# A hybrid two-layer trunk on one core: two matmul stages read last column first, spatial weights interleaved, pooling matmuls halved

## The chip, the core and the metric

The kernel runs on one core of a Trainium2 chip. The metric is the device time of one execution in microseconds (us); lower is better. The engines are TensorE (PE, with its weight loads shown apart as PEld), VectorE (DVE), ScalarE (ACT), GpSimd (POOL) and SyncE (SP), which issues most of the transfers.

## The reference

The input is 512 positions by 1024 features. Two layers follow, each a mixer and a gated FFN with residuals, then a last normalisation. Cut to what matters:

```python
# layer 0
proj = rms_norm(h, norm_mix[0]) @ w_in_even              # 1024 -> 2048
a_b, a_c, a_v, z_b = split(proj, 4)                      # 512 each
y_a = a_b * causal_dwconv3(a_c * a_v, conv_a)
y_b = multiscale_pool(z_b, w_pool, pool_scale)           # 4 groups x (128 -> 128)
h = h + concat(y_a, y_b) @ w_out_even
h = h + gated_conv_ffn(rms_norm(h, norm_ffn[0]), ...)    # 1024 -> 2816 -> 1024
# layer 1
proj = gelu(rms_norm(h, norm_mix[1]) @ w_in_odd)         # 1024 -> 2 x 1024: u, v
ws = w_spatial * tril(ones(128, 128))                    # 8 heads x 128 x 128
gate = einsum('hts,bnshc->bnthc', ws, rms_norm(v, sgu_norm)) + b_spatial
h = h + (u * gate) @ w_out_odd
h = h + gated_conv_ffn(rms_norm(h, norm_ffn[1]), ...)
return rms_norm(h, final_norm)
```

The gated FFN is `silu(conv3(x @ w_gate) + b) * (x @ w_up) @ w_down`.

## The kernel before

All matmul operands are split into a high and a low part in the type float32r: `hi` is the rounded value, `lo` the rest. A product is made of three matmuls (`mm3`, lines 125 to 128): hi by hi, hi by lo, lo by hi, added up in one PSUM bank of 128 x 512 float32. ScalarE makes `hi` (line 121 for weights) and VectorE `lo` (line 122). In a matmul `lhs` is the stationary operand, 128 x 128, which a weight load (LDWEIGHTS) brings into the array, and `rhs` the moving operand, up to 512 columns that stream through it.

The residual `h` stands transposed: eight tiles of 128 features by 512 positions. `hg` holds its normalised parts, hi and lo.

`group` (line 130) computes four output tiles at a time, each in a bank of a rotation of seven (`mm_bank`). It walks over the k tiles with the four outputs inside; for the last `tail` k tiles the order is turned, so that the outputs finish one after another, and `on_done` evicts each. An eighth bank (`aux_bank`) serves small things.

The stages in order, all written out in the program:

- mixer 0: transposes of x, the projections z, ac, av; the pooling matmuls pm (4 groups, one `mm3` each, lines 419 to 422; their stationary operand is the pooling weight, their moving operand the pooled z); the projection ab; the output projection oe.
- FFN of layer 0 (`ffn0`): in two halves, of 12 and 10 tiles of 128 hidden features. Each half has its gate and up matmuls (gu) and then the down-projection, `project` (line 248) under the name d0_0 or d0_12. In a profile its matmuls appear as d: stationary the down weights, moving the gated activations (`a_hi`, `a_lo`), output a transposed residual tile that VectorE adds into `h` (line 266).
- mixer 1: here v and u have the positions in the partitions, so the normalised residual is the stationary operand and the weight the moving one, 512 columns at a time (`in_group` with `lhs_is_weight` false; names v0, v1 and u0, u1, in a profile v and u). The spatial weights `ws` are loaded on ScalarE's queue, masked by GpSimd (line 513), transposed on TensorE in two batches of four heads (wst, line 520) and split into `wsT_hi` by ScalarE (line 523) and `wsT_lo` by VectorE (line 524), two instructions each of 128 x 512. `spatial` (sp) multiplies them, as stationary operands, with the normalised v: per head one `mm3` whose moving operand is four pieces of 128 columns. After the gating come transposes (mT, line 599) and the output projection oo.
- FFN of layer 1 (gu, then dn), with transposes of the residual in between (hT, line 641), and the last normalisation.

Weights come through a ring of four raw buffers of 512 KB, loaded on SyncE's queue; five buffers each hold the hi and lo parts.

Of the kernel before, what the change touches and what calls it, by code (L numbers as in the profile page):

```python
# [9 lines left out]
F32R = mybir.dt.float32r  # L10
# [5 lines left out]
P = 128  # L16
D = 1024
S = 512
NK = D // P
# [11 lines left out]
def tile_trunk(ctx: ExitStack, tc: tile.TileContext, x, norm_mix, norm_ffn, final_norm,  # L31
# [13 lines left out]
    def mm_bank(name):  # L45
        return ps_mm.tile([P, 512], F32, tag="mm", name=name)

    def aux_bank(name):
        return ps_aux.tile([P, 512], F32, tag="aux", name=name)
# [65 lines left out]
    def weights(src, a, b, name):  # L115
        return parts(*fetch(src, a, b, name))
# [5 lines left out]
        nc.vector.tensor_tensor(lo, raw, hi.bitcast(F32), ALU.subtract)  # L122
        return hi, lo

    def mm3(ps, lhs, rhs, start, stop):
        nc.tensor.matmul(ps, lhs[0], rhs[0], start=start, stop=False)  # L126
        nc.tensor.matmul(ps, lhs[0], rhs[1], start=False, stop=False)  # L127
        nc.tensor.matmul(ps, lhs[1], rhs[0], start=False, stop=stop)  # L128

    def group(name, outs, ks, lhs, rhs, tail, on_done, before=None):  # L130

        banks = {}
        head = len(ks) - tail
        order = [(i, j) for i in range(head) for j in outs]
        order += [(i, j) for j in outs for i in range(head, len(ks))]
        at = -1
        for i, j in order:
            if i > at and before is not None:
                before(ks[i])
            at = max(at, i)  # L140
            if j not in banks:
                banks[j] = mm_bank(f"{name}_{j}")
            mm3(banks[j], lhs(ks[i], j), rhs(ks[i], j), i == 0, i == len(ks) - 1)
            if i == len(ks) - 1:
                on_done(j, banks[j])

# [5 lines left out]
    def hg_k(k):  # L152
        return hg[k][0], hg[k][1]
# [64 lines left out]
    def split(pool, src, name, scale=1.0, tag="a", bufs=None):  # L218
        hi = pool.tile([P, S], F32R, tag=f"{tag}hi", bufs=bufs, name=f"{name}_hi")
        lo = pool.tile([P, S], F32R, tag=f"{tag}lo", bufs=bufs, name=f"{name}_lo")  # L220
        nc.scalar.activation(hi, src, AF.Copy, scale=scale)
        if isinstance(scale, float):
            nc.vector.tensor_tensor(lo, src, hi.bitcast(F32), ALU.subtract)
        else:
            nc.vector.scalar_tensor_tensor(lo, src, scale, hi.bitcast(F32),
                                           op0=ALU.mult, op1=ALU.subtract)
        return hi, lo
# [19 lines left out]
    def project(name, w, acts, ks, norm, before=None):  # L247

        for gi in range(2):
            c0 = gi * 512  # L250
            chunks = {}
            for i in range(0, len(ks), 2):
                k0 = min(ks[i], ks[i + 1])
                hi, lo = weights(
                    w[k0 * P : (k0 + 2) * P, c0 : c0 + 512].rearrange("(k p) c -> p k c", p=P),
                    2, 512, f"{name}_{gi}_{k0}")
                chunks[k0], chunks[k0 + 1] = (hi, lo, 0), (hi, lo, 1)

            def lhs(k, j):
                hi, lo, n = chunks[k]  # L260
                cs = slice(j * P, (j + 1) * P)
                return hi[:, n, cs], lo[:, n, cs]

            def done(j, ps):
                k = gi * 4 + j
                nc.vector.tensor_tensor(h[k], ps, h[k], ALU.add)
                if norm is not None:
                    norm.add(k)

            group(f"{name}{gi}", range(4), ks, lhs, lambda k, j: acts[k], 4, done,  # L270
                  before if gi == 0 else None)


    prm0 = prm1 = None
# [1 line left out]
    def in_fetch(name, w, c0, k, n):  # L276
        return fetch(w[k * P : (k + n) * P, c0 : c0 + 512].rearrange("(k p) c -> p k c", p=P),
                     n, 512, f"{name}_{k}")

    def in_parts(chunks, k, raw):  # L280
        hi, lo = parts(*raw)
        for i in range(raw[1]):
            chunks[k + i] = hi[:, i, :], lo[:, i, :]

    def in_group(name, w, c0, lhs_is_weight, on_done, tail, chunks=None, before=None):
        if chunks is None:
            chunks = {}
            for k in range(0, NK, 2):
                in_parts(chunks, k, in_fetch(name, w, c0, k, 2))

        def wt(k, j):
            cs = slice(j * P, (j + 1) * P)
            return chunks[k][0][:, cs], chunks[k][1][:, cs]

        def wt_wide(k, j):
            return chunks[k]

        def tokens(k, j):
            cs = slice(j * P, (j + 1) * P)
            return hg[k][0][:, cs], hg[k][1][:, cs]  # L300

        if lhs_is_weight:
            group(name, range(4), list(range(NK)), wt, lambda k, j: hg_k(k), tail, on_done, before)
        else:
            group(name, range(4), list(range(NK)), tokens, wt_wide, tail, on_done, before)

    def mixer0():
        nonlocal prm0
        w = w_in_even[0]
        with tc.tile_pool(name="m0", bufs=1) as mp:  # L310
# [46 lines left out]
            pooled = {}  # L357
            rstd = [None]

            def z_done(g, ps):  # L360
# [20 lines left out]
                pooled[g] = split(mp, pl, f"pl{g}", tag="mix", bufs=8)  # L381

            in_group("z", w, 1536, True, z_done, 2, zchunks, ahead)
            prm0 = params0()

            wpl = mp.tile([P, 4, P], F32, name="wpl")
            nc.sync.dma_start(wpl, w_pool[0].rearrange("g c d -> c g d"))
            wpl_hi = mp.tile([P, 4, P], F32R, name="wpl_hi")
            wpl_lo = mp.tile([P, 4, P], F32R, name="wpl_lo")
# [5 lines left out]
            def c_done(j, ps):  # L395
# [5 lines left out]
                ac[j] = t  # L401

            in_group("ac", w, 512, True, c_done, 4)

            cv = {}

            def v_done(j, ps):
# [7 lines left out]
                cv[j] = t  # L415

            in_group("av", w, 1024, True, v_done, 4)

            for g in range(4):
                ps = mm_bank(f"pm{g}")  # L420
                mm3(ps, (wpl_hi[:, g, :], wpl_lo[:, g, :]), pooled[g], True, True)
                mix[4 + g] = split(mp, ps, f"yb{g}", scale=prm0("psc", g), tag="mix", bufs=8)

            def b_done(j, ps):
# [4 lines left out]

            nxt = Norm("f0", lambda k: prm0("ffn", k))  # L430
            project("oe", w_out_even[0], mix, [4, 5, 6, 7, 0, 1, 2, 3], nxt)
            return nxt

# [55 lines left out]
    def ffn0(norm):  # L489
        nonlocal prm1  # L490
        with tc.tile_pool(name="f0", bufs=1) as ap:
            rstd = lazy_rstd(norm)
            nxt = None
            for a, b in HALVES:
                acts = {}
                for f in range(a, b, 2):
                    gate_up(0, prm0, rstd, ap, acts, f, 4 if f == 0 else NK)
                if b == NF:
                    prm1 = params1()
                    nxt = Norm("m1", lambda k: prm1("mix", k))  # L500
                project(f"d0_{a}", w_ffn_down[0], acts, list(range(a, b)), nxt)
            return nxt


    def mixer1(norm):
        w = w_in_odd[0]
        with tc.tile_pool(name="m1", bufs=1) as mp:
# [4 lines left out]
            nc.scalar.dma_start(ws, w_spatial[0].rearrange("h t s -> t h s"))  # L512
            nc.gpsimd.affine_select(out=ws, in_=ws, pattern=[[0, NK], [-1, P]],
                                    compare_op=ALU.is_ge, fill=0.0, base=0, channel_multiplier=1)
            wsT_hi = mp.tile([P, NK, P], F32R, name="wsT_hi")
            wsT_lo = mp.tile([P, NK, P], F32R, name="wsT_lo")
            for q in range(2):
                ps = aux_bank(f"wst{q}")
                for i in range(4):
# [14 lines left out]
            v = [mp.tile([P, D], F32, tag="v", bufs=4, name=f"v{t}") for t in range(NT)]  # L534
# [39 lines left out]
            def spatial(j):  # L574
                ps = mm_bank(f"sp{j}")
                cs = slice(j % 4 * P, (j % 4 + 1) * P)
                mm3(ps, (wsT_hi[:, j, :], wsT_lo[:, j, :]),
                    (vn[j // 4][0][:, :, cs], vn[j // 4][1][:, :, cs]), True, True)
                if j % 2 == 0:
                    gt["pair"] = mp.tile([P, 2, S], F32, tag="v", bufs=4, name=f"gt{j}")  # L580
                g = by_chunk(gt["pair"][:, j % 2, :])
                nc.vector.tensor_tensor(
                    g, by_chunk(ps),
                    g_bc[:, :, j * P : (j + 1) * P].to_broadcast([P, NT, P]), ALU.mult)
                gt[j] = g
# [37 lines left out]

            nxt = Norm("f1", lambda k: prm1("ffn", k))
            project("oo", w_out_odd[0], mix, list(range(NK)), nxt, before=second_half)
            return nxt

# [70 lines left out]
    def group8(name, ks, lhs, rhs, tail, on_done):  # L698
# [4 lines left out]
        for i, j in order:  # L703
# [3 lines left out]
            if i == len(ks) - 1:  # L707
                on_done(j, banks[j])

    n = mixer0()  # L710
    n = ffn0(n)
    n = mixer1(n)
    ffn1(n)

# [29 lines left out]
```

## Time and profile before

| | |
|---|---|
| median of 3 runs | 1022.07 us (1020.68 to 1022.85) |
| profiled execution, time | 1023.1 us |
| profiled execution, span | 1021.4 us |
| mean granted TensorE clock | 0.998 |
| TensorE busy | 1009.4 us, 99% of the span |
| VectorE, ScalarE, GpSimd busy | 559.0, 345.3, 126.7 us |
| moved by DMA | 101.24 MB, mean 99 GB/s |

The span is the time from the first to the last instruction of the profiled execution; the time holds what lies around it too. A matmul's record contains its latency, and records of consecutive matmuls overlap: their cost is read from the distance of their starts. The chain of waits is followed back from the last instruction; each piece in it is the time that it adds.

In groups and timelines a row has: line, engine, operation, output <- inputs (buffer numbers left out), array tile and shape, count; then the busy time in us, the mean duration of one in ns, and the idle time of the engine just before, with its releaser.

### The profile page before, as it was taken

What the parts mean: (1) busy time and instruction counts of PE and PEld (TensorE: products, weight loads), DVE (VectorE), ACT (ScalarE), POOL (GpSimd) and SP (SyncE); (2) the same over time, 40 slices, a digit from 0 to 9 for tenths busy, and PEclk for the clock granted to TensorE, in tenths of its full rate; (3) what the DMA queues carried; (4) which work ended last, traced back from release to release, by engine and by line L of the source; (5) the groups of instructions that cost most, each with busy time, mean ns of one, the idle gap of its engine ahead of it and who ended that gap; (6) DMA issues with size and microseconds to landing.
All of it is one profiled execution on the core that took longest, in us unless ns stands there. A gap on an engine that the chain in (4) does not pass through costs nothing.

```text
span 1021.4 us, 11177 instructions
## 1 busy us (share of the span) xinstructions
PE 1009.4 (99%) x4485; PEld 832.4 (81%) x4485; DVE 559.0 (55%) x706; ACT 345.3 (34%) x449; POOL 126.7 (12%) x113
## 2 busy tenths in 40 slices
PE   9999999999999999999999999999999999999997
PEld 6788888888888888888878888888888888888885
DVE  5997567755623455654423645486554226565526
ACT  5423443323312223333345444433332212332313
POOL 3141121111100011111110001211111001111100
PEclk9999999999999999999999999999999999999999
DMA  7432233332333332332333123324233224233302
GB/s 232 154 103 83 83 103 98 92 115 89 95 111 84 96 109 83 103 104 78 106 126 103 62 91 96 103 83 124 83 103 103 84 81 124 83 104 103 100 3 83
DMA packets 74719, 101.24 MB, mean 99 GB/s; under 512 B 3268, under 2 KB 52652, under 8 KB 74668
## 3 DMA queue, kind: packets, MB, share of 16 engines
q1 hardware_dynamic: 73324, 98.96, 31.2%
q10 hardware_dynamic: 1344, 1.58, 0.5%
q8 instruction: 35, 0.57, 0.2%
q14 instruction: 16, 0.13, 0.0%
HBM read 98.42 MB, written 2.10 MB: 98 GB/s over the span
## 4 chain that ended last, share of the span: by engine, by line
PE 97%; DVE 1%; DMA 1%; issue 0%; POOL 0%; ACT 0%; DVEq 0%; POOLq 0%; ACTq 0%
PE gu L127 16%; PE gu L128 16%; PE gu L126 16%; PE dn L127 4%; PE d L126 4%; PE d L128 4%; PE dn L128 4%; PE d L127 4%; PE dn L126 4%; PE oo L128 1%; PE u L127 1%; PE u L126 1%; PE oo L127 1%; PE u L128 1%; PE oe L127 1%; PE oe L126 1%
## 5 line engine op out<-in xcount | busy, mean ns | idle before, releaser
L126 PE MATMUL gu<-hgh,whi_g 128*128 128x512 f32 x352 | 137.3, 390 | 0.0
L128 PE MATMUL gu<-hgh,wlo_g 128*128 128x512 f32 x352 | 137.0, 389 | 0.0
L128 PE MATMUL gu<-hgh,wlo_u 128*128 128x512 f32 x352 | 137.0, 389 | 0.0
L127 PE MATMUL gu<-hgl,whi_g 128*128 128x512 f32 x352 | 136.9, 389 | 0.0
L126 PE MATMUL gu<-hgh,whi_u 128*128 128x512 f32 x352 | 136.9, 389 | 0.0
L127 PE MATMUL gu<-hgl,whi_u 128*128 128x512 f32 x352 | 136.9, 389 | 0.0
L470 POOL TENSOR_TENSOR s<-s,rstd_f 128x512 f32<-128x512 f32 x44 | 66.5, 1512 | 529.8 <-ACT s L469 529.8
L121 ACT ACTIVATE whi_g<-raw_g 128x1024 fp32r<-128x1024 f32 x44 | 46.6, 1059 | 169.9 <-PE gu L127 107.8
L122 DVE TENSOR_TENSOR wlo_u<-raw_u,whi_u 128x1024 fp32r<-128x1024 f32 x52 | 63.8, 1229 | 59.5 <-ACT whi_u L121 59.1
L122 DVE TENSOR_TENSOR wlo_g<-raw_g,whi_g 128x1024 fp32r<-128x1024 f32 x44 | 54.4, 1236 | 47.3 <-ACT whi_g L121 46.9
L126 PEld LDWEIGHTS gu<-hgh,whi_u 128*128 128x128 f32 x352 | 66.1, 188 | 13.8
L127 PEld LDWEIGHTS gu<-hgl,whi_u 128*128 128x128 f32 x352 | 66.1, 188 | 13.7
L128 PEld LDWEIGHTS gu<-hgh,wlo_g 128*128 128x128 f32 x352 | 66.1, 188 | 13.7
L126 PEld LDWEIGHTS gu<-hgh,whi_g 128*128 128x128 f32 x352 | 66.1, 188 | 13.6
L128 PEld LDWEIGHTS gu<-hgh,wlo_u 128*128 128x128 f32 x352 | 66.1, 188 | 13.6
L127 PEld LDWEIGHTS gu<-hgl,whi_g 128*128 128x128 f32 x352 | 66.1, 188 | 13.6
L121 ACT ACTIVATE whi_u<-raw_u 128x1024 fp32r<-128x1024 f32 x52 | 55.0, 1059 | 58.6 <-PE gu L127 20.7
L126 PE MATMUL d<-a_hi,whi_d 128*128 128x512 f32 x176 | 68.6, 390 | 0.0
L128 PE MATMUL d<-a_hi,wlo_d 128*128 128x512 f32 x176 | 68.5, 389 | 0.0
L127 PE MATMUL d<-a_lo,whi_d 128*128 128x512 f32 x176 | 68.5, 389 | 0.0
L126 PE MATMUL dn<-whi_dn,a_hi 128*128 128x512 f32 x176 | 68.5, 389 | 0.0
L127 PE MATMUL dn<-wlo_dn,a_hi 128*128 128x512 f32 x176 | 68.5, 389 | 0.0
(236 smaller groups left out, 1772.5 us busy)
## 6 DMA issues: line engine op xcount, KB each, us to landing
raw_g<-in_w_ffn_gate_dram SPq DMA_DIRECT2D x44, 512.0 KB
raw_u<-in_w_ffn_up_dram SPq DMA_DIRECT2D x44, 512.0 KB, 3.9
raw_d<-in_w_ffn_down_dram SPq DMA_DIRECT2D x22, 512.0 KB, 3.5
raw_dn<-in_w_ffn_down_dram SPq DMA_DIRECT2D x22, 512.0 KB, 3.3
raw_oe<-in_w_out_even_dram SPq DMA_DIRECT2D x8, 512.0 KB, 3.3
raw_v<-in_w_in_odd_dram SPq DMA_DIRECT2D x8, 512.0 KB, 3.6
raw_u<-in_w_in_odd_dram SPq DMA_DIRECT2D x8, 512.0 KB, 3.5
raw_oo<-in_w_out_odd_dram SPq DMA_DIRECT2D x8, 512.0 KB, 3.3
```

Source lines behind the costliest of these rows:

```text
L121: nc.scalar.activation(hi, raw, AF.Copy)
L122: nc.vector.tensor_tensor(lo, raw, hi.bitcast(F32), ALU.subtract)
L126: nc.tensor.matmul(ps, lhs[0], rhs[0], start=start, stop=False)
L127: nc.tensor.matmul(ps, lhs[0], rhs[1], start=False, stop=False)
L128: nc.tensor.matmul(ps, lhs[1], rhs[0], start=False, stop=stop)
L470: nc.gpsimd.tensor_tensor(s, s, r, ALU.mult)
```

## The change

`back` makes an access pattern that walks the last dimension from its last element to its first. `mm3` gets an argument `turned`: where it is set, the moving operand and the PSUM output are both walked that way, so each column still lands at its place. It is set for the d stage (names that begin with d0) and for the v stage (names that begin with v). Second, the four pooling products are made in two halves of 256 columns each, with the same weights. Third, `wsT_hi` and `wsT_lo` become one tile whose last dimension of two holds the hi and the lo part side by side, so either is read and written with a step of two elements.

```diff
--- before.py
+++ after.py
@@ -122,12 +122,20 @@
         nc.vector.tensor_tensor(lo, raw, hi.bitcast(F32), ALU.subtract)
         return hi, lo
 
-    def mm3(ps, lhs, rhs, start, stop):
+    def back(ap):
+
+        step, n = ap.ap[-1]
+        return bass.AP(tensor=ap.tensor, offset=ap.offset + step * (n - 1),
+                       ap=[*ap.ap[:-1], [-step, n]])
+
+    def mm3(ps, lhs, rhs, start, stop, turned=False):
+        if turned:
+            ps, rhs = back(ps), [back(r) for r in rhs]
         nc.tensor.matmul(ps, lhs[0], rhs[0], start=start, stop=False)
         nc.tensor.matmul(ps, lhs[0], rhs[1], start=False, stop=False)
         nc.tensor.matmul(ps, lhs[1], rhs[0], start=False, stop=stop)
 
-    def group(name, outs, ks, lhs, rhs, tail, on_done, before=None):
+    def group(name, outs, ks, lhs, rhs, tail, on_done, before=None, turned=False):
 
         banks = {}
         head = len(ks) - tail
@@ -140,7 +148,8 @@
             at = max(at, i)
             if j not in banks:
                 banks[j] = mm_bank(f"{name}_{j}")
-            mm3(banks[j], lhs(ks[i], j), rhs(ks[i], j), i == 0, i == len(ks) - 1)
+            mm3(banks[j], lhs(ks[i], j), rhs(ks[i], j), i == 0, i == len(ks) - 1,
+                turned)
             if i == len(ks) - 1:
                 on_done(j, banks[j])
 
@@ -268,7 +277,7 @@
                     norm.add(k)
 
             group(f"{name}{gi}", range(4), ks, lhs, lambda k, j: acts[k], 4, done,
-                  before if gi == 0 else None)
+                  before if gi == 0 else None, name.startswith("d0"))
 
 
     prm0 = prm1 = None
@@ -302,7 +311,8 @@
         if lhs_is_weight:
             group(name, range(4), list(range(NK)), wt, lambda k, j: hg_k(k), tail, on_done, before)
         else:
-            group(name, range(4), list(range(NK)), tokens, wt_wide, tail, on_done, before)
+            group(name, range(4), list(range(NK)), tokens, wt_wide, tail, on_done, before,
+                  name.startswith("v"))
 
     def mixer0():
         nonlocal prm0
@@ -418,7 +428,10 @@
 
             for g in range(4):
                 ps = mm_bank(f"pm{g}")
-                mm3(ps, (wpl_hi[:, g, :], wpl_lo[:, g, :]), pooled[g], True, True)
+                for n in range(2):
+                    cs = slice(n * 256, (n + 1) * 256)
+                    mm3(ps[:, cs], (wpl_hi[:, g, :], wpl_lo[:, g, :]), [a[:, cs] for a in pooled[g]],
+                        True, True)
                 mix[4 + g] = split(mp, ps, f"yb{g}", scale=prm0("psc", g), tag="mix", bufs=8)
 
             def b_done(j, ps):
@@ -512,8 +525,8 @@
             nc.scalar.dma_start(ws, w_spatial[0].rearrange("h t s -> t h s"))
             nc.gpsimd.affine_select(out=ws, in_=ws, pattern=[[0, NK], [-1, P]],
                                     compare_op=ALU.is_ge, fill=0.0, base=0, channel_multiplier=1)
-            wsT_hi = mp.tile([P, NK, P], F32R, name="wsT_hi")
-            wsT_lo = mp.tile([P, NK, P], F32R, name="wsT_lo")
+            wsT = mp.tile([P, NK, P, 2], F32R, name="wsT")
+            wsT_hi, wsT_lo = wsT[:, :, :, 0], wsT[:, :, :, 1]
             for q in range(2):
                 ps = aux_bank(f"wst{q}")
                 for i in range(4):
```

## The prediction

> **What bounds the kernel now.** I read the page's first two parts and its chain of waits.
>
> ```profile
> span 1021.4 us, 11177 instructions
> PE 1009.4 (99%) x4485; PEld 832.4 (81%) x4485; DVE 559.0 (55%) x706; ACT 345.3 (34%) x449; POOL 126.7 (12%) x113
> PEclk9999999999999999999999999999999999999999
> PE 97%; DVE 1%; DMA 1%; issue 0%; POOL 0%; ACT 0%; DVEq 0%; POOLq 0%; ACTq 0%
> ```
>
> TensorE is busy 99% of the span at a granted clock of 0.9 or more in every slice, and the chain that ended last is 97% TensorE. A longer matmul step therefore reaches the end at once; a longer VectorE or ScalarE instruction mostly does not. Next come the groups by line and shape, for the matmuls that the change touches and their weight loads (PEld).
>
> ```profile
> L126 PE MATMUL d<-a_hi,whi_d 128*128 128x512 f32 x176 | 68.6, 390 | 0.0
> L128 PE MATMUL d<-a_hi,wlo_d 128*128 128x512 f32 x176 | 68.5, 389 | 0.0
> L127 PE MATMUL d<-a_lo,whi_d 128*128 128x512 f32 x176 | 68.5, 389 | 0.0
> L126 PE MATMUL v<-whi_v,hgh 128*128 128x512 f32 x64 | 25.1, 392 | 0.0
> L128 PE MATMUL v<-whi_v,hgl 128*128 128x512 f32 x64 | 25.0, 391 | 0.0
> L127 PE MATMUL v<-wlo_v,hgh 128*128 128x512 f32 x64 | 24.9, 389 | 0.0
> L126 PE MATMUL sp<-vnh,wsT_hi 128*128 128x512 f32 x8 | 3.1, 389 | 0.0
> L126 PE MATMUL pm<-pl_hi,wpl_hi 128*128 128x512 f32 x4 | 1.6, 389 | 0.0
> L126 PEld LDWEIGHTS sp<-vnh,wsT_hi 128*128 128x128 f32 x8 | 1.5, 188 | 0.3
> ```
>
> Turned round are 3 x 176 = 528 matmuls of d (the FFN down-projection of layer 0) and 3 x 64 = 192 of v (the gating input of layer 1): 720. In the built program all 720 have step -1 in both the moving operand and the PSUM output, so the change does what it says. The other edits touch 3 x 8 = 24 spatial loads (sp) and 3 x 4 = 12 pooling matmuls (pm). No group has idle time before it. The 389 ns are a record with its latency; what a matmul costs is the distance between starts, which the TensorE timeline (d stage, 20 matmuls) and the chain in order of time (sp stage, 24 matmuls; z, the first projection) show:
>
> ```profile
> 299.62 0.39 PE L127 MATMUL d<-a_lo,whi_d 128*128 128x512 f32 x1
> ...
> 303.93 0.39 PE L128 MATMUL d<-a_hi,wlo_d 128*128 128x512 f32 x1
> ```
>
> ```profile
> 9.43 0.43 PE z L127
> ...
> 576.73 0.23 PE sp L126
> ...
> 581.94 0.23 PE sp L128
> ```
>
> (303.93 - 299.62) / 19 = 0.227 us a step in d. In sp it is (581.94 - 576.73) / 23 = 0.227 as well, although there the moving operand jumps: four pieces of 128 columns, 512 elements apart. The z row, 0.43 us, is the longest full-width step that stands in the chain by itself; it belongs to the first projection's first matmuls.
>
> **The turned matmuls.** No row of before has a descending step, so its price is bounded. Below: no full-width step of the trace is shorter than about 0.227, and descending order takes no column, load or instruction away, so I see no mechanism for a gain beyond noise; 720 x 0 = 0. Above: the z step, 0.43; 720 x (0.43 - 0.227) = 146 us. Between ends so far apart I take the row that it is nearest to: sp, whose read is also irregular along the free dimension and which costs nothing. A descending run touches the same consecutive words as an ascending one, in the other order. The value taken is 0.
>
> The Trainium skill's page "SBUF — State Buffer", section "SBUF: two separate sides", says that SBUF serves 16-byte lines, and that a read runs at full rate when at least two consecutive accesses fall into one line. Descending 4-byte columns have four to a line: by that rule the extra is 0 too. No run here shows a descending read.
>
> Were the turned matmuls slower, one small wait would shrink. It is the only TensorE wait in these stages, shown here in the chain and in the list of waits:
>
> ```profile
> 507.56 0.24 PE d L128
> 507.82 0.70 DVE h L266
> 508.55 0.01 ACT hgh L164
> 508.55 5.87 DMA ws<-in_w_spatial_dram
> 514.57 1.97 POOL ws L513
> 516.58 0.66 PE wst L520 x4
> PE wst L520 <- POOL ws L513: 1.5, 1, 1.5
> ```
>
> The transposes of the spatial weights (wst) stand in TensorE's queue behind the first v matmuls and wait 1.5 us for the masked weights. The transfer starts when the d stage ends, so it shifts with d; but v work ahead of wst that gets longer fills the wait. From the end of the last d matmul (507.8) to 515.0, where it falls idle (516.58 - 1.55), are some 32 steps of 0.227. A v matmul longer by over 1.5 / 32 = 0.047 us fills the whole 1.5 us.
>
> **The interleaved spatial weights.** Instruction counts stay; 24 loads read their columns 8 bytes apart instead of 4. A load takes 0.188 us beside a matmul step of 0.227, so 0.039 us are free. Bounds: 0, if the load keeps its time; if it doubles, 2 x 0.188 - 0.227 = 0.149 us stick out of each, 24 x 0.149 = 3.6 us. I take 0: a load may grow by a fifth and still be hidden. The two producing instructions also write with that step:
>
> ```profile
> L523 ACT ACTIVATE wsT_hi<-wst x2: 597/597/597, 517.3 to 519.3; 128x512 fp32r<-128x512 f32 x2
> L524 DVE TENSOR_TENSOR wsT_lo<-wst,wsT_hi x2: 691/691/691, 517.9 to 520.0; 128x512 fp32r<-128x512 f32 x2
> PEld wst L520 <- DVE wsT_lo L524: 0.2, 1, 0.2
> ```
>
> The consumer, sp, comes 56 us after them (576.7), which hides them. But the second batch of transposes needs the one auxiliary bank back and already waits 0.2 us for the first VectorE instruction; both doubled would put 0.6 + 0.7 = 1.3 us on TensorE. I take 0 (these writes are 128x512, paced per element in the nearest rows), and keep 1.3 for the range.
>
> **The pooling matmuls.** 12 steps of 0.227 (2.7 us) become 24 half-width ones, each with its own weight load. The nearest narrow steps are in the chain:
>
> ```profile
> 528.18 0.79 PE ssc_m L193 x8
> 588.52 0.24 PE u L128
> 695.18 0.87 PE hT L641 x8
> ```
>
> hT is 8 loads with 128 columns each in 0.87 us, 0.109 a step; ssc is 8 loads with one column each in 0.79, 0.099 a step. So a load-and-matmul pair can follow another after 0.1 us, and loads alone do not hold a half-width step up. A straight line from 128 columns (0.109) to 512 (0.227) gives 0.148 at 256: 24 x 0.148 - 2.7 = +0.8 us. Exactly half a step gives 0; a half that costs a whole step gives +2.7. I take +0.4, between the first two. ScalarE's eviction of pm comes that much later, and after pm stand 96 matmuls of the next projection (ab), 22 us, before TensorE needs anything made from it.
>
> The same tiles get thirteen new waits of TensorE on itself (oe, gu, v, u and sp: for earlier matmuls into the bank they take over). Behind such a wait stands all of TensorE's queue, but the bank was last written at least four output tiles back in a rotation of seven; before has three such waits in front of oo and three in front of ac, and no TensorE wait on PE is in its list of waits. I take 0.
>
> **Sum.** 0 + 0 + 0.4 + 0 = +0.4 us. The profiled execution took 1023.1 us with a span of 1021.4, 1.0 above the median of the three runs, 1022.07 (1020.68 to 1022.85). By its own time the forecast is 1023.5; against the median, which I forecast, 1022.5. A difference of about 0.2% (2.0 us) is what a measurement of this kernel can tell from none. The forecast's own range is 1020.5 to 1026: down by the spread of the runs, up by half of the bounds above (3.6 + 1.3 + 2.7 = 7.6).
>
> **Rivals.**
> Half rate: the array's column stream moves several columns at a time, and a descending order breaks the grouping at the read or at the PSUM write, so that every turned matmul takes about twice the step. Place: d and v, 720 steps. Price: 0.43 each, +146 less the 1.5 us of the wst wait and with the 0.4, so 1022.1 + 145 = 1167; a full doubling (0.454) gives 720 x 0.227 = 163, 1184. Against it is that sp's jumps are free; for it that sp keeps runs of 128 ascending columns, so the trace never tests the order inside a run, and that the output is turned too, which nothing in the trace resembles. It decides from very little: with no slack on TensorE, 2.0 / 720 = 0.0028 us a matmul, 1.2% of a step, is already slower than can be told from noise.
>
> The Trainium skill's page "PSUM — Partial Sum Buffer", section "Specifications (TRN2)", says that PSUM has 8-byte lines and that any non-contiguous pattern slows matmuls significantly. [...]
>
> A fixed toll: a turned matmul starts or ends later by a small amount, the stream itself keeping its rate. The trace's small disturbances are of that kind: the u row above has 0.24 instead of 0.227 after transposes. 720 x 0.013 = 9 us, 1032; with 0.08 a matmul 58 - 1.5, 1079.
>
> Worse than double: a turned matmul goes by more than two steps' time, over 1186. Only the size speaks against it: no 512-column step in the trace is near that.
>
> The small edits alone at their upper bounds: +7.6 us, 1030, with the turned matmuls free.
>
> Faster: it would need a turned step under 0.224. Nothing in the trace is for it.
>
> **How the numbers follow.** No change (the forecast) 0.36: the nearest row is for it, but it rests on a row that does not test the order inside a run. Half rate 0.28; fixed toll 0.17; worse than double 0.08; small edits alone above 2 us 0.05; faster 0.06. The largest single case is no change, though the slower ones together weigh more: slower 0.28 + 0.17 + 0.08 + 0.05 = 0.58, within 0.2% 0.36, faster 0.06. The range must take in the half rate to leave out no more than 2 in 10 (without it 0.42 would be outside): 1020.5 to 1186 holds 0.36 + 0.05 + 0.17 + 0.28 = 0.86.
>
> **What would show it.** In the profile after: starts of d and v matmuls 0.227 apart as in the untouched gu stage means the main step was right; 0.24 to 0.31 is the toll, 0.43 or more the half rate, and then the wait of wst for POOL is gone. sp starts 0.227 apart means the interleaved loads are hidden; over that, they stick out. pm in about 3.1 us rather than 2.7 means the halves were sized right. The forecast is wrong if d and v differ from gu by over 0.003 us a step.

## The result, and the profile after

The changed kernel takes 1027.13 us (median of 9 runs, 1025.95 to 1031.62), before 1022.47 in the same comparison (9 runs, 1020.54 to 1023.45). The ratio is 1.0053, 95% interval [1.0038, 1.0068]: about 4.7 us slower, which is more than the 0.2% that a measurement of this kernel can tell from none.

The page of the changed kernel, its first parts. `mm3` has moved by eight lines, so L134 to L136 are what L126 to L128 were before.

```profile
span 1029.9 us, 11203 instructions
PE 1015.6 (99%) x4497; PEld 834.3 (81%) x4497; DVE 559.1 (54%) x706; ACT 345.6 (34%) x449; POOL 125.8 (12%) x113
PEclk9999999999999999999999999999999999999999
PE 97%; DMA 1%; DVE 1%; issue 0%; POOL 0%; ACT 0%; SPq 0%; DVEq 0%; POOLq 0%; ACTq 0%
```

TensorE still bounds the kernel at the same granted clock; VectorE and ScalarE are as busy as before. This profiled execution is the slowest of the nine (1031.62 us), so its span is not the result; stage by stage it still tells where the time went. The groups of the changed stages:

```profile
L134 PE MATMUL d<-a_hi,whi_d 128*128 128x512 f32 x176 | 70.0, 398 | 0.0
L135 PE MATMUL d<-a_lo,whi_d 128*128 128x512 f32 x176 | 69.9, 397 | 0.0
L135 PE MATMUL v<-wlo_v,hgh 128*128 128x512 f32 x64 | 25.4, 397 | 0.0
L134 PE MATMUL sp<-vnh,wsT 128*128 128x512 f32 x8 | 3.2, 394 | 0.0
L134 PE MATMUL pm<-pl_hi,wpl_hi 128*128 128x256 f32 x8 | 2.3, 282 | 0.0
L134 PEld LDWEIGHTS d<-a_hi,whi_d 128*128 128x128 f32 x176 | 33.1, 188 | 8.0
L134 PEld LDWEIGHTS sp<-vnh,wsT 128*128 128x128 f32 x8 | 1.5, 193 | 0.3
```

The mean d matmul has gone from 389 ns to 397, sp from 389 to 394, and the interleaved load from 188 to 193; the load in d has kept its 188. Starts tell the cost. In the TensorE timeline of the d stage these are the first and the last of 19 matmuls, then the same for v:

```profile
299.65 0.40 PE L134 MATMUL d<-a_hi,whi_d 128*128 128x512 f32 x1
...
303.86 0.40 PE L134 MATMUL d<-a_hi,whi_d 128*128 128x512 f32 x1
...
540.71 0.40 PE L134 MATMUL v<-whi_v,hgh 128*128 128x512 f32 x1
...
544.91 0.40 PE L134 MATMUL v<-whi_v,hgh 128*128 128x512 f32 x1
```

4.21 / 18 and 4.20 / 18 give 0.2333 to 0.234 us a step, against 0.2267 before (in d, 18.14 us over 80 steps). From the chain in order of time, pm (23 steps between these rows) and sp (the first and the last of its 24):

```profile
82.42 0.12 PE pm L134
...
85.17 0.12 PE pm L136
...
585.05 0.23 PE sp L134
...
590.41 0.23 PE sp L136
```

A half-width pooling matmul takes 2.75 / 23 = 0.120, and an sp step 5.36 / 23 = 0.233. The sum: 720 x 0.0067 = 4.8 us from the turned matmuls, 24 x 0.120 - 12 x 0.227 = +0.16 from pooling, 24 x 0.0064 = +0.15 from the spatial weights, 5.1 in all, inside the interval of the ratio (3.9 to 7.0 us).

The rest of the 8.5 us by which the two profiled spans differ lies in the first stage and in one transfer. The list of waits and the chain:

```profile
PE wst L533 <- POOL ws L526: 2.7, 1, 2.7
PE xt_ps L341 <- DMA xt<-in_x_dram: 1.6, 1, 1.6
514.52 8.08 DMA ws<-in_w_spatial_dram
```

After the wait of 1.6 us for the input, z began 0.9 us later than before, and ten of its steps instead of three took 0.43 us, so its last matmul started at 38.93 instead of 36.66. The transfer of the spatial weights took 8.08 us instead of 5.87, and TensorE waited 2.7 us for them instead of 1.5. Neither is tied to the change. With the turned matmuls alone and with the small edits alone (both below), the last z matmul starts at 36.86 and 36.02, and the wst wait is in neither list of waits; with nearly every product turned it is 1.5 again. That wait differs between profiled executions, so the 1.5 us of before is no fixed term either.

### The profile page after: what moved, and what is told of

Its sections match the earlier page's. It is cut to its first block, busy times and chain, and to the rows that moved or that the text cites. A ratio compares the mean times of both kernels' runs of the same rounds, so it can differ in the third digit from the quotient of the medians.

```text
span 1029.9 us, 11203 instructions
## 1 busy us (share of the span) xinstructions
PE 1015.6 (99%) x4497; PEld 834.3 (81%) x4497; DVE 559.1 (54%) x706; ACT 345.6 (34%) x449; POOL 125.8 (12%) x113
## 4 chain that ended last, share of the span: by engine, by line
PE 97%; DMA 1%; DVE 1%; issue 0%; POOL 0%; ACT 0%; SPq 0%; DVEq 0%; POOLq 0%; ACTq 0%
PE gu L135 16%; PE gu L134 15%; PE gu L136 15%; PE d L134 4%; PE d L135 4%; PE d L136 4%; PE dn L134 4%; PE dn L135 4%; PE dn L136 4%; PE u L134 1%; PE oo L134 1%; PE u L136 1%; PE oo L135 1%; PE u L135 1%; PE oo L136 1%; PE oe L135 1%
## 5 line engine op out<-in xcount | busy, mean ns | idle before, releaser
L134 PE MATMUL gu<-hgh,whi_g 128*128 128x512 f32 x352 | 137.3, 390 | 0.0
L136 PE MATMUL gu<-hgh,wlo_g 128*128 128x512 f32 x352 | 137.0, 389 | 0.0
L136 PE MATMUL gu<-hgh,wlo_u 128*128 128x512 f32 x352 | 137.0, 389 | 0.0
L134 PE MATMUL gu<-hgh,whi_u 128*128 128x512 f32 x352 | 136.9, 389 | 0.0
L134 PEld LDWEIGHTS gu<-hgh,whi_u 128*128 128x128 f32 x352 | 66.1, 188 | 13.8
L136 PEld LDWEIGHTS gu<-hgh,wlo_g 128*128 128x128 f32 x352 | 66.1, 188 | 13.8
L136 PEld LDWEIGHTS gu<-hgh,wlo_u 128*128 128x128 f32 x352 | 66.1, 188 | 13.7
L134 PEld LDWEIGHTS gu<-hgh,whi_g 128*128 128x128 f32 x352 | 66.1, 188 | 13.7
L134 PE MATMUL d<-a_hi,whi_d 128*128 128x512 f32 x176 | 70.0, 398 | 0.0
L136 PE MATMUL d<-a_hi,wlo_d 128*128 128x512 f32 x176 | 69.9, 397 | 0.0
L134 PE MATMUL dn<-whi_dn,a_hi 128*128 128x512 f32 x176 | 68.5, 389 | 0.0
```

## The experiments

**The parts apart.** The first kernel turns d and v and leaves pooling and spatial weights as they were; the second has these two edits and turns nothing.

> Both sides turned in the d and v stages, pooling and spatial weights as before. If the turned matmuls carry the change, starts in d and v lie 0.233 us apart as in the changed kernel, and 720 x 0.0066 = 4.8 us come on top of before: ratio about 1.0047. If the two small edits carried it (the rival), the ratio is 1.000 and the starts 0.227.

> Pooling in halves and spatial weights interleaved, no matmul turned. If the turned matmuls carry the change: 24 x 0.120 - 12 x 0.227 = +0.16 us for pooling and 24 x 0.0064 = +0.15 us for the spatial matmuls, ratio 1.0003, not to be told from 1. If the small edits carried it: 1.005.

The turned matmuls alone give a ratio of 1.0045, [1.0032, 1.0059] (1026.48 us against 1021.98); the two small edits alone 1.0001, [0.9991, 1.0011]. The turned matmuls carry the change. The second kernel's profile still has steps of 0.120 in pm and 0.2333 in sp.

**Read or write.** In `mm3` of the first kernel one of the two sides is left ascending:

```diff
-            ps, rhs = back(ps), [back(r) for r in rhs]
+            rhs = [back(r) for r in rhs]          # the read alone
+            ps = back(ps)                         # or the PSUM output alone
```

> In d and v only the moving operand is read last column first, the PSUM output ascends, so each product's columns come out mirrored. Theory that the toll is at the read: starts 0.233 apart, ratio 1.0047. Theory that it is at the PSUM write: 0.227, 1.000. If each side has a part of it, in between.

> In d and v only the PSUM output runs from its last column to its first, the moving operand ascends, so each product's columns come out mirrored. Theory that the toll is at the read: starts 0.227 apart, ratio 1.000. Theory that it is at the PSUM write: 0.233, 1.0047.

The read alone: 1.0047, [1.0035, 1.0060]. The output alone: 1.0000, [0.9991, 1.0008]. Starts of d in the two timelines, the read alone first, 18 steps each:

```profile
299.73 0.40 PE L135 MATMUL d<-a_lo,whi_d 128*128 128x512 f32 x1
...
303.93 0.40 PE L135 MATMUL d<-a_lo,whi_d 128*128 128x512 f32 x1
```

```profile
299.79 0.39 PE L135 MATMUL d<-a_lo,whi_d 128*128 128x512 f32 x1
...
303.87 0.39 PE L135 MATMUL d<-a_lo,whi_d 128*128 128x512 f32 x1
```

0.2333 and 0.2267. The whole toll sits at the descending read of the moving operand; a descending PSUM output costs nothing. So the rule of the Trainium skill's page "PSUM — Partial Sum Buffer", section "Specifications (TRN2)", that a non-contiguous pattern slows matmuls, does not reach to a descending one here. The Trainium skill's page "Advanced Engine Details and Errata", section "PSUM Cachelines", has the same rule, and adds that every two consecutive elements should be contiguous for best throughput; descending pairs are, and this run (1.0000) agrees with that second sentence, not with the first.

**Every stage.** `mm3` turns every product whose moving operand is one plain run.

> All 4332 matmuls with a plain moving operand of the three-part products are turned on both sides, not only the 720 of d and v; pooling and spatial weights as before. A toll per turned matmul: 4332 x 0.0066 = 28.6 us, 1050.6, ratio 1.028, with 0.233 in every stage. If the toll belongs to the d and v stages alone (their tiles, their neighbours): about 1.005.

1049.82 us, ratio 1.0271, [1.0254, 1.0288], where 1.028 was expected. In the untouched gu stage of before the step was 0.2267; here, 18 steps:

```profile
259.61 0.40 PE L135 MATMUL gu<-hgl,whi_u 128*128 128x512 f32 x1
...
263.81 0.40 PE L135 MATMUL gu<-hgl,whi_g 128*128 128x512 f32 x1
```

0.2333 again. The toll is the same whichever tiles are read, and adds up over 4332 matmuls.

**Width.** In `group`, for the named stages, each product is made in pieces; `cut(a, b, True)` turns both sides of columns a to b.

```diff
+        "d0_00": [cut(0, 256, True), cut(256, 512, True)],
+        "d0_01": [cut(0, 256), cut(256, 512)],
+        "d0_120": [cut(0, 258), cut(258, 512)],
+        "d0_121": [cut(0, 258, True), cut(258, 512, True)],
+        "v0": [cut(n * 128, (n + 1) * 128, True) for n in range(4)],
+        "v1": [cut(n * 128, (n + 1) * 128) for n in range(4)],
```

> The same columns in narrower matmuls, turned and ascending side by side; each product of three matmuls is a sum of its own, so the sums over k are left out in d and v. First half of d: outputs 0 to 3 in two turned halves of 256 columns, outputs 4 to 7 in two ascending ones. Second half of d: pieces of 258 and 254 columns, ascending, then turned, so that pieces begin in the middle of a 16-byte line. v: turned quarters of 128, then ascending ones. Theory of a fixed toll per matmul: 256 ascending 0.120, turned 0.1266. Theory of a toll per column: 256 turned 0.1233 (half of 0.0066 more). Theory that the toll comes from the place in its line where a read begins: the ascending piece that begins at column 258 pays it too, and the turned one that begins there does not pay the same as the one that begins at 511. At 128 columns, 128/512 of the stream of 0.213 plus 0.013 is 0.067, under the 0.1 that loads take one after another in the trace of before, so turned and ascending come out alike at about 0.1 if loads set the pace.

The timeline at 256 columns, turned (52 steps), then ascending (51 steps):

```profile
289.82 0.28 PE L132 MATMUL d<-a_hi,whi_d 128*128 128x256 f32 x1
...
295.97 0.28 PE L133 MATMUL d<-a_lo,whi_d 128*128 128x256 f32 x1
```

```profile
329.80 0.28 PE L132 MATMUL d<-a_hi,whi_d 128*128 128x256 f32 x1
...
335.92 0.28 PE L132 MATMUL d<-a_hi,whi_d 128*128 128x256 f32 x1
```

0.1183 turned and 0.1200 ascending: at half width the descending read costs nothing, and is even 0.0017 shorter. Both theories written down fall, the fixed toll (0.1266) and the toll per column (0.1233). The pieces of 258 and 254 columns, some of which begin in the middle of a 16-byte line, give 0.1200 turned and 0.1198 ascending over the whole stretch. Since no toll shows at this width, they do not tell whether the place in the line plays a part at 512 columns: that theory stays untested. The quarters tell little of the toll, because the granted clock fell in that stage (last section).

A scan over eleven splits was to tell the shape of the width dependence:

> The gate and up matmuls of both layers in two pieces of N and 512 - N columns, N = 512, 496, 480, 448, 416, 384, 352, 320, 288, 272, 264 from group to group; layer 0 turned, layer 1 ascending; each product of three is a sum of its own, so sums over k are left out in these stages. Read is the distance from one N-column matmul to the next inside a product. Ascending: 0.120 at 256 and 0.2267 at 512 give 0.4167 ns a column and 13.3 ns fixed. Turned: 0.1183 and 0.2333. Theory of a dearer column: 0.449 ns a column and a fixed part of 3.3 ns, on a straight line over all widths, crossing the ascending one near 300 columns. Theory of a threshold: turned like ascending up to a width near 512 and then a jump by 0.0067. Theory of rounding: the turned step moves in steps of 0.0067 (0.120 is 18 of them, 0.2267 34, 0.2333 35) that do not coincide with the ascending ones.

At 512 columns it shows 0.2333 and 0.2267 once more. At unequal splits the steps inside a product scatter (at 384 columns from 0.174 to 0.257), so no single-width price can be read; that the narrow piece, paced by its loads, shifts the starts of the wide one is likely but not shown. Whole products of two pieces differ little by direction: 0.867 us turned against 0.864 ascending at 384 + 128, 0.780 against 0.774 at 320 + 192, 0.710 against 0.713 at 272 + 240. Over the ten splits the difference lies between -0.003 and +0.007; three full-width matmuls differ by 0.020. The scan did not settle between the theories.

**Some of the three.** Only a share of the d matmuls is turned.

```diff
+        "d0_00": lambda j: (0,),
+        "d0_01": lambda j: (1,),
+        "d0_120": lambda j: (0, 1),
+        "d0_121": lambda j: (0, 1, 2) if j % 2 else (),
```

> Both sides turned, but only some of the three matmuls of a product: in the first half of d the first alone (outputs 0 to 3), then the second alone (4 to 7); in the second half the first two (0 to 3), then all three in every other output tile (4 to 7); in v the third alone, then the last two. Toll bound to each turned matmul: the mean step is 0.2267 plus 0.0067 times the turned share: 0.2289 with one in three, 0.2311 with two, 0.2300 with every other product. Toll bound to the reversal between neighbours (an ascending one before or behind a turned one): none or another price where directions change, so one in three is not a third of the toll. Toll that takes hold of a whole stream: 0.2333 as soon as some are turned.

First and last rows of two of the four stretches of d in the timeline, the first of the three turned (138 steps) and the first two turned (107 steps):

```profile
279.14 0.39 PE L137 MATMUL d<-a_hi,wlo_d 128*128 128x512 f32 x1
...
310.99 0.39 PE L137 MATMUL d<-a_hi,wlo_d 128*128 128x512 f32 x1
...
454.73 0.40 PE L137 MATMUL d<-a_lo,whi_d 128*128 128x512 f32 x1
...
479.81 0.39 PE L137 MATMUL d<-a_hi,whi_d 128*128 128x512 f32 x1
```

31.85 / 138 = 0.2308 with the first of the three turned; the second gave 0.2289; the first two 25.08 / 107 = 0.2344, more than all three (0.2333); every other product 0.2325. In v, between neighbouring v matmuls, the third alone gave about 0.231 and the last two 0.233. A third of the matmuls costs a third or almost two thirds of the toll, depending on which. The toll is therefore no property of the turned matmul alone: the neighbours' directions come into it.

**Interleaved loads in numbers, and both at once.** High and low weights of gate and up lie interleaved, as the spatial weights did; layer 0 is also turned.

```diff
+            both = wp.tile([P, a, b, 2], F32R, tag="wboth", bufs=5, name=f"wb_{name}")
+            hi, lo = both[:, :, :, 0], both[:, :, :, 1]
```

> The weights of gate and up in both layers with high and low parts interleaved, as the spatial weights were (2 x 1056 loads with step 2); in layer 0 these matmuls are also turned on both sides. Nothing else is changed, d and v ascend. Layer 1: 0.2333 a step if the toll that 24 spatial matmuls paid holds for any load. Layer 0: if turning and interleaving each pay, 0.240, and the whole is 1056 x (0.0133 + 0.0067) = 21 us, ratio 1.0207; if they share one step of rounding, 0.2333 and 2112 x 0.0067 = 14 us, ratio 1.0138. If the spatial toll was peculiar to that stage: layer 1 at 0.2267, 7 us, 1.0069.

1035.77 us, ratio 1.0124, [1.0103, 1.0145]: the 14 us of the shared step (1.0138), not the 21 of two tolls (1.0207). Layer 0, then layer 1, 18 steps each:

```profile
199.71 0.40 PE L139 MATMUL gu<-hgl,wb_g 128*128 128x512 f32 x1
...
203.91 0.40 PE L139 MATMUL gu<-hgl,wb_u 128*128 128x512 f32 x1
...
879.62 0.40 PE L140 MATMUL gu<-hgh,wb_u 128*128 128x512 f32 x1
...
883.82 0.39 PE L140 MATMUL gu<-hgh,wb_u 128*128 128x512 f32 x1
```

0.2333 in both. A descending read, an interleaved load, and the two together all lengthen the full-width step by the same 0.0067. That is what rounding to a grid would do: 0.1200, 0.2267 and 0.2333 are 18, 34 and 35 times 0.00667. The runs are consistent with this grid and rule out that the two tolls add; what in the hardware makes it, and why half-width turned matmuls (0.1183) and mixed products (0.2289, 0.2308) leave it, stays open.

**Other steps.** Moving operands of 4-byte columns read with steps 2, -2, 3 and 4, and one head's weights with step 4.

> Other steps than 1 and -1 of 4-byte columns; the products are other ones than the reference's in d, v and the spatial stage. First half of d: halves of 256 columns read with step 2, then with step -2, output ascending. v: 512 columns with step 2 over two weight rows, then step -2. Spatial stage: heads 0 and 1 read the moving operand with step 4 (a 16-byte line per column), 6 and 7 with step 3, heads 3 to 5 as before, head 2 loads weights with step 4. Theory that the toll belongs to any step other than 1: steps 2 and 3 cost 0.233 at 512 columns, 0.1266 at 256. Theory that only the descending direction pays: step 2 costs 0.227 and step -2 0.233. Theory of lines (two columns to a line are free, fewer are not): steps 2 and -2 as 1 and -1, steps 3 and 4 far longer, 0.3 to 0.43. The interleaved weights (step 2) paid 0.0064 a load; weights with step 4 then pay 0.0064 again (any step) or far more (lines).

Timeline of v with step 2 (14 steps) and with step -2 (13 steps):

```profile
597.63 0.64 PE L132 MATMUL v<-whi_v,hgh 128*128 128x512 f32 x1
...
603.96 0.63 PE L134 MATMUL v<-whi_v,hgl 128*128 128x512 f32 x1
```

```profile
639.81 0.65 PE L132 MATMUL v<-whi_v,hgh 128*128 128x512 f32 x1
...
645.87 0.65 PE L133 MATMUL v<-wlo_v,hgh 128*128 128x512 f32 x1
```

0.452 and 0.466: a step of 2 doubles the time, and the descending one adds to it. In sp, six steps each, step 3 gives 0.445 and step 4 0.458, so from 2 on the size of the step hardly matters. At 256 columns step 2 costs 0.230, against 0.120 with step 1, and step -2 costs 0.2333 (30 steps between these rows), so here the direction has a price at half width too:

```profile
344.70 0.41 PE L133 MATMUL d<-a_lo,whi_d 128*128 128x256 f32 x1
...
351.70 0.41 PE L133 MATMUL d<-a_lo,whi_d 128*128 128x256 f32 x1
```

The half rate that the prediction put on descending order exists, but for skipped columns. None of the three theories foresaw it: the toll of 0.0067 for any step and the toll for descending alone both put step 2 far below 0.45, and the theory of lines had it free. The rule of the Trainium skill's page "SBUF — State Buffer", section "SBUF: two separate sides", that two hits on a 16-byte line are enough, therefore does not hold here for the moving operand: step 2 has two columns to a line. The weights read with step 4 had loads of 0.31 us in their records instead of 0.19, yet their matmul steps stayed at 0.23 to 0.25.

## Why the prediction was right or wrong

The forecast, no change at 1022.5, was wrong; of its rivals the fixed toll came in. The stated range, 1020.5 to 1186, holds 1027.13 only because it was stretched to take in the half rate, which did not come; the forecast's own range, 1020.5 to 1026, misses it. The step that failed is the value 0 for the turned matmuls, taken from sp "whose read is also irregular": sp's runs of 128 ascending columns say nothing on the order inside a run, which the prediction itself named as what spoke for a rival. The term is 720 x 0.0067 = 4.8 us. It lies above the point of decision (0.0028 a matmul) and at half the price that the toll had at its lower end (0.013, from the 0.24 after transposes).

That the toll is "fixed" held as a price where the change put it: 0.0067 a full-width matmul in every stage. As a mechanism it is not shown: at a single width an addition at the start or end looks the same as a slower stream, half-width matmuls do not pay it, and mixed directions pay other shares.

Half rate and worse did not occur. The half-rate rival put the break at the read or at the PSUM write; the output turned out free (1.0000), and the read keeps almost its whole rate. By the rule of the Trainium skill's page "SBUF — State Buffer", quoted in the prediction, the extra was 0; measured is 0.0067. The row that gave the upper bound, z with 0.43, need not be a price of the access order: z reads ascending columns, and in the run with interleaved gate and up weights ascending v matmuls took the same 0.43 between 524 and 526 us, where the granted clock was 0.52. For z itself the profile shows a clock of 1.00, so what slowed it stays open.

Pooling: sized at +0.4 (bounds 0 and +2.7), measured +0.16, as 24 steps of 0.120. The straight line from the fp32 transposes had 0.148; the true steps are half the full stream plus the same fixed part (0.0133 us, worked out from 0.120 and 0.2267), so loads of 0.19 us in their records do not pace them.

Interleaved weights: taken as 0 because 0.039 us of the step were free for the load. The load grew by 0.005 only, and the step still by 0.0064 (24 x 0.0064 = 0.15 us); room in the record was not room in the step. The writing instructions, from 597 to 638 ns on ScalarE and from 691 to 692 on VectorE, cost far less than the bound of 1.3 us.

The new waits of TensorE on itself: none is among TensorE's waits in the profile after. The wst wait, said to shrink in slower cases: 32 x 0.0067 = 0.2 us could have been filled. Between profiles it ranges from none (turned matmuls alone) over 1.5 (before) to 2.7 us (the changed kernel), so nothing of those 0.2 us can be made out.

## What to carry to other kernels

When one engine holds the whole chain and its step repeats thousands of times, an access pattern that no row of the profile shows needs a price of its own, and 1% of a step is enough to decide. A row that is irregular in another way, jumps between runs, does not stand in for order or spacing inside a run. Read and write sides are told apart in one comparison, by turning each alone.

## What the runs showed of the hardware that was not expected

A moving operand of 4-byte columns with a step of 2 halves TensorE's rate (0.452 us for 512 columns, 0.2267 with step 1), while weights loaded with a step of 2 cost 0.0067 a matmul. Two causes that each lengthen a step by 0.0067 do not add.

In the v stage in quarters of 128 columns the granted clock fell. A wait of TensorE, then three stretches from the view of busy time by stretch (columns: stretch, its length, then busy time of PE, PEld, DVE, ACT and POOL with counts, granted clock, DMA share, GB/s):

```profile
PE wst L547 <- POOL ws L540: 5.8, 1, 5.8
514.00:518.00 4.00, 4.00 (x38) 3.98 (x36) 3.52 (x4) 2.65 (x4) 0.93 (x1) 1.00 0.58 160
564.00:640.00 76.00, 76.00 (x358) 76.00 (x358) 4.50 (x8) 11.35 (x18) 0.00 (x0) 0.50 0.07 25
688.00:690.00 2.00, 2.00 (x10) 1.68 (x9) 1.05 (x5) 1.16 (x3) 0.00 (x0) 1.00 0.70 241
```

Up to 518 us the quarters ran at the full clock with 0.11 us a step, so four of them took 0.44 where one full-width matmul takes 0.2267. Then TensorE waited 5.8 us for the masked spatial weights, and afterwards the clock was 0.50 and a quarter took 0.213 us, turned or ascending, until v ended at 684 us, although TensorE was busy for the whole of the second stretch. It was back at 1.00 by 688 us, after 4 us of full-width matmuls of u. In the run with interleaved gate and up weights a wait of 2.0 us at the same place was followed by a clock of 0.52 as well, but there full-width matmuls stood behind it and the clock was 1.00 again 4 us later. So the fall came after a stop, and it lasted while the matmuls were narrow; that the narrow matmuls kept the clock down fits both runs, but no run changes the width alone after the same stop.
